# Pinned tiled runs in a chunked recurrence, and convolutions ahead of operand splits: one step of a hybrid decoder layer on one core

## The chip, the cores and the metric

The kernel runs on one core of one Trainium2 chip. The metric is the device time of one execution in microseconds, and the number that stands for a kernel is the median of its runs: 1178.71 us for the kernel before, from 3 runs between 1177.01 and 1179.49.

## The reference

One layer of a decoder is applied to a prompt of 512 tokens and to a sample group of 8 sequences with 8 tokens each, 576 tokens in all. Both groups use the same weights. Cut to its core:

```python
xn = rmsnorm(x, g_norm)
u, za, xb, zb, q, zc, gates = split_in(xn @ w_in)          # w_in: 1024 x 11392
oa, s_last, shift_last = rwkv7_branch(u, za, ...)          # 16 heads of 64
ob, h_last, conv_last = rglru_branch(xb, zb, ...)          # width 1024
oc = cross_attn(q, zc, mem_k, mem_v)                       # 4 heads, 256 memory tokens
g_a, g_b, g_c = split(sigmoid(gates), 3)
merged = g_a * (oa @ w_br_a) + g_b * (ob @ w_br_b) + g_c * (oc @ w_br_c)
y = x + merged @ w_out                                     # then a last rmsnorm
```

The RWKV-7 branch carries, for each head, a 64 x 64 state over the tokens:

```python
sa = einsum("bhvk,bhk->bhv", s, -kk_t)
s = s * w_t[:, :, None, :] + sa[..., None] * (kk_t * a_t)[:, :, None, :] + v_t[..., None] * k_t[:, :, None, :]
o_t = einsum("bhvk,bhk->bhv", s, r_t)
```

The RG-LRU branch is a convolution of width 4 over the tokens, two gates made by block-diagonal products of its result, and the scan h = a_t * h + b_t. The outputs are y for both groups, the last states, and the memory's keys and values.

## The kernel before

**Projections.** Every weight matrix is used in units of 128 columns (class Unit, L310). A unit's weights are loaded in one DMA of 512 KB (raw), rounded on ScalarE to a high part (whi, L293), and the rest is made on VectorE (wlo, L294). The activations xh and xl are split the same way, and a product is three matmuls: high by high, high by low, low by high. A unit is eight steps, one for each 128 rows of the contraction; a step for all tokens is six matmuls of 288 columns (L366 to L369). The class Stream (L318) holds the units in order. `st.go(n)` puts n steps into the program at that place, `st.until(label)` puts as many as are needed until that unit is through, and `st.add` puts units ahead of the others that wait. At the first step of a unit the next unit's weights are loaded. So the projections are the filler that is woven between everything else: u, k, r, v of the recurrence, its gate za, and a list of units whose results are put aside in DRAM (zb, g, xb, zc; L449).

**The order of the work.** The program is written in one order, and a scheduler then orders each engine's instructions from a model of their times: an instruction that is not ready in its model lets later ones go ahead. On TensorE, `K.mm` and `K.transpose` (L63, L69) can pin an instruction: while `K.pin` is set, each is held behind the instruction that was traced just before it on that engine. Before the change `K.pin` is set in `lru_phase` alone (L571 to L611), and the stream's steps, which use `K.mm` too, are pinned there with the rest. In the recurrence nothing is pinned, and most of its matmuls call `nc.tensor.matmul` directly.

**The recurrence** (`rwkv_phase`, L861) goes over four groups of two pairs of heads (G = 2, L863), and turns the token-by-token recurrence into nine chunks of 64 tokens, the ninth being the 64 sample tokens. Names, for one pair o:

- `prep_a` (L958) and `prep_b` (L985) make the decays and the scaled keys and reads, in tiles BK and ZR; `rs` (L991) is a row sum in column tiles.
- `prep_c` (L1022) scales BK to BKn by each chunk's decay, transposes v and BKn (`vt`, `bkt`, whole matmuls), and at its end makes the products M1 (`m`, L1049: tiles of 64 x 64 of the array, evacuated with a mask by VectorE at L1055).
- `invert` (L1059) sends the diagonal 32 x 32 blocks of M1 through DRAM (d1) to a layout in which VectorE inverts all of them at once by 30 substitution steps (L1072 to L1077), and sends the result back (d2, d3).
- `direct` (L1115) makes products that do not need the inverse (R, Zt); `bonus` (L1011) one more term.
- `invert2` (L1094) completes the inverse with tiles of 32 x 32 (`z`, `w`), `solved` (L1141) applies it (`U`, `W`, tiles of 64 x 64).
- `chain` (L1182) is one chunk: A, two whole matmuls from the state (L1187), VectorE's addition of A to UV (`plus_state`, L1177), dS (L1196) and the outputs (`outs`, L1167, which add to A), both in column tiles of 64, and VectorE's addition of dS to the state sbd (L1204). GpSimd scales the state for the next chunk meanwhile (L1189). Two steps of the stream are put after A and four after the outputs.
- `sample_a`, `sample_b`, `sample_c` (L1222 to L1272) treat the ninth chunk, with eight separate states: transposes of the loaded states (whole), A8 in column tiles of 32 (L1248) and dSs in column tiles of 64 (L1261), transposes and stores. They follow chunks 1 to 3 for the first pair and 4 to 6 for the second.

After chunk 7 come the za units, the group norm, `prep_a` of the next group, and the output of the branch.

**The LRU phase** (`lru_phase`, L482). Just before it, all eight tiles of the attention branch's output are loaded from DRAM (SyncE's queue) and split to high and low parts on ScalarE and VectorE (`load_split`, L474, called at L1512). Then, pinned: a convolution (`conv`, L502; its input xe comes by a DMA on ScalarE's queue, then one ScalarE and four VectorE passes), 8 steps, the next convolution, 6 steps, the first `gates` (`pg`, L531), and so on, until the last g unit is through; then the branch products (`br`) begin, first with the attention branch's split output.

The instructions of a float32 matmul are two in the profile, so the eight dS of a chunk are four matmuls.

Of the kernel before, what the change touches and what calls it, by code (L numbers as in the profile page):

```python
# [9 lines left out]
F32 = mybir.dt.float32  # L10
# [8 lines left out]
P = 128  # L19
D = 1024  # L20
KC = 8
# [296 lines left out]
class Stream:  # L318


    def __init__(self, K):
        self.K = K
        self.first, self.fill = [], []
        self.cur = self.nxt = None
        self.k = 0
        self.done = set()

# [15 lines left out]
    def step(self):  # L343
# [138 lines left out]
def lru_phase(K, o2, merge, operand):  # L482
# [6 lines left out]
    with tc.tile_pool(name="lruc", bufs=1, reuse_waits="tile") as lc, tc.tile_pool(name="lru", bufs=2, reuse_waits="tile") as lp:  # L489
# [121 lines left out]
        K.pin = False  # L611
# [249 lines left out]
def rwkv_phase(K):  # L861
# [5 lines left out]
    with ExitStack() as es:  # L867
# [90 lines left out]
        def prep_a(o):  # L958
# [5 lines left out]
            for s in range(2):  # L964
                cs = slice(HN * s, HN * s + HN)
                for n, (dst, bias) in enumerate(((tw, K.w0h), (ta, K.a0h))):
                    pl = K.psb("lora")[:, 0:HN]
                    nc.tensor.matmul(pl, wlh[:, n, :], xw2[n][:, cs], start=True, stop=False)
                    nc.tensor.matmul(pl, wll[:, n, :], xw2[n][:, cs], start=False, stop=True)
# [15 lines left out]
        def prep_b(o):  # L985
# [4 lines left out]
            for c in range(NCH):  # L990
                nc.tensor.matmul(pr_[br:br + 64, 2 * c:2 * c + 2], o.sq[:, C * c:C * c + C], K.bones2, start=True, stop=True,  # L991
                                 tile_position=(0, br))
# [18 lines left out]
        def bonus(o):  # L1011
# [3 lines left out]
            for s in range(2):  # L1015
                cs = slice(HN * s, HN * s + HN)
                pb = K.psb("bon")[:, 0:HN]
                nc.tensor.matmul(pb, K.bones, hi[:, cs], start=True, stop=False)
                nc.tensor.matmul(pb, K.bones, lo[:, cs], start=False, stop=True)
                nc.vector.tensor_mul(o.bon[:, cs], pb, o.v[:, cs])  # L1020

        def prep_c(o):  # L1022
            q, BK, ZR = o.q, o.BK, o.ZR
            rv = rsv[q]
            UV = o.UV = UV2[0][:, q]
            BKn = o.BKn = rg.tile([P, NCH, P], F32, tag="BKn", name="BKn")
            for c in range(8):
# [3 lines left out]
                                 o.Ps[:, :, NS:NS + 1].unsqueeze(1).to_broadcast([P, 2, NB, NS]))  # L1031
            for c0, n in ((0, 4), (4, 4), (8, 1)):
# [10 lines left out]
            M1 = o.M1 = rg.tile([P, H2, P], F32, tag="M1", name="M1")  # L1043
            for c0, n in ((0, 4), (4, 4), (8, 1)):
                pms = [K.psb("m1") for h in range(2)]
                for c in range(c0, c0 + n):
                    for w in range(2):
                        for h in range(2):
                            nc.tensor.matmul(pms[h][64 * w:64 * w + 64, P * (c - c0):P * (c - c0) + P],  # L1049
                                             BK[64 * h:64 * h + 64, c, w, :],  # L1050
                                             ZR[64 * h:64 * h + 64, c].rearrange("p a b -> p (a b)"), start=True, stop=True,
                                             tile_position=(64 * h, 64 * w))
                for h in range(2):
                    for c in range(c0, c0 + n):
                        nc.vector.scalar_tensor_tensor(M1[:, 2 * c + h, :], pms[h][:, P * (c - c0):P * (c - c0) + P],  # L1055
                                                       rv[:, c, h:h + 1], maskq[q][c == 8],
                                                       op0=ALU.mult, op1=ALU.mult)

        def invert(prs):  # L1059

            d1 = dr.tile([NQ, 32, 32], F32, tag="d1", name="d1")
            for blk in range(2):
                for o in prs:
                    q0 = (blk * G + o.q) * H2
                    nc.sync.dma_start(d1[q0:q0 + H2].rearrange("q s t -> s q t"),
                          o.M1[o.br + 32 * blk:o.br + 32 * blk + 32, :, o.br + 32 * blk:o.br + 32 * blk + 32])
# [3 lines left out]
            nc.sync.dma_start(X, d1)  # L1070
# [23 lines left out]
        def invert2(prs):  # L1094
            for g0 in (0, 9):
                pzs = [K.psb("z1") for o in prs]
                for g in range(g0, g0 + 9):
                    for o, pz in zip(prs, pzs):
                        a, b = o.br, o.br + 32
                        nc.tensor.matmul(pz[b:b + 32, 32 * (g - g0):32 * (g - g0) + 32], o.M1[a:a + 32, g, b:b + 32],  # L1100
                                         o.xz[a:a + 32, g, :], start=True, stop=True, tile_position=(a, b))
                for o, pz in zip(prs, pzs):
                    b = o.br + 32
                    nc.scalar.copy(o.xz[b:b + 32, g0:g0 + 9, :].rearrange("p a b -> p (a b)"), pz[b:b + 32, 0:288])
                pws = [K.psb("w12") for o in prs]
                for g in range(g0, g0 + 9):
                    for o, pw in zip(prs, pws):
                        a, b = o.br, o.br + 32
                        nc.tensor.matmul(pw[a:a + 32, 32 * (g - g0):32 * (g - g0) + 32], o.xz[b:b + 32, g, :],
                                         o.M1[b:b + 32, g, b:b + 32], start=True, stop=True, tile_position=(b, a))  # L1110
                for o, pw in zip(prs, pws):
                    a, b = o.br, o.br + 32
                    nc.scalar.copy(o.M1[a:a + 32, g0:g0 + 9, b:b + 32], pw[a:a + 32, 0:288].rearrange("p (a b) -> p a b", b=32))

        def direct(prs):  # L1115

            r0 = prs[0].r0 = [rt.tile([P, N], F32, tag="k", name="r0") for _ in range(2)]
            for c0, n in ((0, 4), (4, 4), (8, 1)):
                pR = K.psb("R")
                for c in range(c0, c0 + n):  # L1120
                    for h in range(2):
                        for o in prs:
                            a, b, m = o.kr, o.br, P * (c - c0) + C * h
                            nc.tensor.matmul(pR[b:b + 64, m:m + C], o.M1[a:a + 64, 2 * c + h, b:b + 64],
# [448 lines left out]
```

## Time and profile before

| What | Value |
|---|---|
| median of 3 runs | 1178.71 us |
| the profiled execution's own time | 1175.92 us |
| its span, first to last instruction | 1174.2 us |
| mean granted TensorE clock | 0.992 |
| TensorE matmul busy | 1135.5 us |
| VectorE busy | 709.0 us |
| ScalarE busy | 521.2 us |
| HBM read, written | 120.82 MB, 29.01 MB |

Engines are called PE (TensorE's matmuls), PEld (its weight loads), DVE (VectorE), ACT (ScalarE), POOL (GpSimd) and SP (SyncE); a q behind a name is the engine's sequencer, which issues DMAs. Rows of the timeline give the start in us from the span's start, the length in us, the engine, the line of the kernel, the operation, what it writes and reads, the rows and columns of the array that a matmul uses (128*128 is the whole array), its shape, and how many instructions of the kind follow one another. In square brackets stands the engine's idle time before, and what ended it. Matmuls overlap in TensorE's pipeline, so the pace is read from one start to the next, not from the lengths.

### The profile page before, as it was taken

The page shows a single profiled execution, that of the slowest core. Times are in us where ns is not written, and L with a number is a line of the kernel's source. Part 1 is how long each engine was busy: PE and PEld are TensorE (multiplying, and loading weights), DVE is VectorE, ACT ScalarE, POOL GpSimd, SP SyncE. Part 2 cuts the span into 40 slices and gives each one's busy share as a digit, 9 for nine tenths or more (in the row PEclk, how much of TensorE's full clock was granted, in tenths as well). Part 3 has the DMA queues.
Part 4 walks back from the last instruction along what each step waited for, and adds up shares of the span by engine and source line. Part 5 has one row for each costly group of instructions (what it writes and reads, how often), then busy time and mean ns, then how long its engine had stood idle before and what let it go on. Part 6 is the DMA issues. An engine that isn't in the chain of part 4 may idle for free.

```text
span 1174.2 us, 25723 instructions
## 1 busy us (share of the span) xinstructions
PE 1135.5 (97%) x10567; PEld 1064.0 (91%) x10567; DVE 709.0 (60%) x1454; ACT 521.2 (44%) x1004; POOL 148.0 (13%) x287
## 2 busy tenths in 40 slices
PE   6999999999999999999999999999999799999997
PEld 4998988899899899998899988989989799999997
DVE  5345655245883478745686745879445669684633
ACT  5454444245523365324472244642323677622333
POOL 3010000011002210003210022100121012020032
PEclk9999999999999999999999999999999899999999
DMA  5456757632334223352223423234544846566412
GB/s 141 130 198 198 223 181 233 199 101 64 95 116 113 73 66 91 109 152 55 65 86 101 132 76 76 76 97 127 139 114 136 261 134 206 151 218 179 126 37 81
DMA packets 220622, 151.49 MB, mean 129 GB/s; under 512 B 52640, under 2 KB 196106, under 8 KB 220506
## 3 DMA queue, kind: packets, MB, share of 16 engines
q1 hardware_dynamic: 217242, 146.87, 42.7%
q10 hardware_dynamic: 3264, 2.99, 0.9%
q8 instruction: 83, 1.36, 0.5%
q14 instruction: 33, 0.27, 0.1%
HBM read 120.82 MB, written 29.01 MB: 128 GB/s over the span
## 4 chain that ended last, share of the span: by engine, by line
PE 79%; DVE 6%; DMA 5%; ACT 5%; issue 4%; SPq 0%; POOL 0%; DVEq 0%; ACTq 0%; POOLq 0%
PE u L71 13%; PE g L71 12%; PE br L71 11%; PE xb L71 4%; PE za L71 4%; PE fo L71 4%; PE q L71 4%; PE zc L71 3%; PE zb L71 3%; PE kv L71 2%; PE pg L71 1%; PE m L1049 1%; DVE wlo L294 1%; PE dS L1196 1%; PE skt L65 1%
## 5 line engine op out<-in xcount | busy, mean ns | idle before, releaser
L293 ACT CAST whi<-wraw 128x1024 fp32r<-128x1024 f32 x129 | 135.2, 1048 | 313.8 <-PE g L71 91.1
L294 DVE TENSOR_TENSOR wlo<-wraw,whi 128x1024 fp32r<-128x1024 f32 x128 | 158.1, 1235 | 117.1 <-ACT whi L293 108.1
L71 PE MATMUL u<-xh,whi 128*128 128x288 f32 x400 | 92.5, 306 | 0.0
L71 PE MATMUL u<-xh,wlo 128*128 128x288 f32 x400 | 89.9, 301 | 0.0
L71 PE MATMUL u<-xl,whi 128*128 128x288 f32 x400 | 88.2, 300 | 0.0
L71 PE MATMUL g<-xh,whi 128*128 128x288 f32 x384 | 85.7, 304 | 0.0
L71 PE MATMUL g<-xl,whi 128*128 128x288 f32 x384 | 84.4, 300 | 0.0
L71 PE MATMUL g<-xh,wlo 128*128 128x288 f32 x384 | 84.1, 299 | 0.0
L71 PE MATMUL br<-oh,wlo 128*128 128x288 f32 x384 | 82.7, 297 | 1.4 <-DVE wlo L294 1.4
L71 PE MATMUL br<-oh,whi 128*128 128x288 f32 x384 | 83.6, 299 | 0.0
L71 PE MATMUL br<-ol,whi 128*128 128x288 f32 x384 | 82.3, 296 | 0.0
L71 PEld LDWEIGHTS u<-xh,whi 128*128 128x128 f32 x400 | 65.0, 188 | 6.2 <-issue 4.7
L71 PEld LDWEIGHTS u<-xh,wlo 128*128 128x128 f32 x400 | 65.1, 188 | 1.8 <-issue 0.8
L71 PEld LDWEIGHTS u<-xl,whi 128*128 128x128 f32 x400 | 64.6, 189 | 0.6 <-issue 0.2
L71 PEld LDWEIGHTS g<-xh,whi 128*128 128x128 f32 x384 | 62.4, 190 | 1.5 <-issue 1.0
L71 PEld LDWEIGHTS br<-oh,wlo 128*128 128x128 f32 x384 | 61.8, 189 | 1.9 <-DVE wlo L294 1.8
L71 PEld LDWEIGHTS g<-xh,wlo 128*128 128x128 f32 x384 | 62.4, 189 | 1.2 <-issue 1.2
L71 PEld LDWEIGHTS g<-xl,whi 128*128 128x128 f32 x384 | 62.4, 189 | 1.1 <-issue 1.0
L71 PEld LDWEIGHTS br<-oh,whi 128*128 128x128 f32 x384 | 62.2, 189 | 0.6
L71 PEld LDWEIGHTS br<-ol,whi 128*128 128x128 f32 x384 | 61.9, 189 | 0.0
L1075 DVE TENSOR_TENSOR Xt<-X 72x30 f32<-72x30 f32 (+14 forms) x120 | 39.3, 327 | 12.9 <-DMA X<-d 9.2
L71 PE MATMUL fo<-woh,oh 128*128 128x256 f32 (+1 forms) x160 | 44.9, 280 | 0.0
(392 smaller groups left out, 2856.4 us busy)
## 6 DMA issues: line engine op xcount, KB each, us to landing
wraw<-in_w_in SPq DMA_DIRECT2D x89, 512.0 KB
wraw<-in_w_mem_kv SPq DMA_DIRECT2D x16, 512.0 KB
kn<-in_cache_mem_k SPq DMA_DIRECT2D x16, 512.0 KB
kn<-in_cache_mem_v SPq DMA_DIRECT2D x16, 512.0 KB
gd<-flt SPq DMA_DIRECT2D x24, 288.0 KB
gtt<-gd SPq DMA_DIRECT2D x24, 288.0 KB
wraw<-in_w_br_c SPq DMA_DIRECT2D x8, 512.0 KB
wraw<-in_w_br_a SPq DMA_DIRECT2D x8, 512.0 KB
```

The lines of the kernel that those rows point to most:

```text
L65: ins = self.nc.tensor.transpose(out, in_, self.ident[:rows, :rows])
L71: ins = self.nc.tensor.matmul(*a, **kw)
L293: nc.scalar.copy(hi, raw)
L294: eng.tensor_sub(lo, raw, hi.bitcast(F32))
L1049: nc.tensor.matmul(pms[h][64 * w:64 * w + 64, P * (c - c0):P * (c - c0) + P], BK[64 * h:64 * h + 64, c, w, :], ZR[64 * h:64 * h + 64, c].r ...
L1075: nc.vector.tensor_mul(tv, X[:, 0:s, s:s + 1].to_broadcast([NQ, s, m]), X[:, s:s + 1, s + 1:].to_broadcast([NQ, s, m]))
L1196: nc.tensor.matmul(pS[hs, C * o.q:C * o.q + C], o.BKn[:, c, hs], o.UV[:, c, hs], start=True, stop=True, tile_position=(0, 64 * h))
```

## The change

In the recurrence:

- From `bonus` to the end of chunk 7, `K.pin` is set, and the recurrence's matmuls go through `K.mm`, so each is held behind what was traced just before it. The stream's steps have a pin of their own, `st.pin`, which is set only in the LRU phase.
- `chain` takes two functions. `full()` is traced behind A: the sample's transposes. `tiled()` is traced behind the outputs: A8, the sample's outputs and dSs. The sample's parts move by that: its outputs and dSs stand a chunk behind A8, its states are loaded ahead of chunk 0 and behind chunk 3, and `sample_c` of the second pair comes after chunk 7.
- The steps in a chunk are 2 and 4 as before, but 1 and 3 in the last group.
- `prep_c` is cut in three. `scaled` (BKn) and `products` (M1, and the DMA of its blocks to d1, per pair) come right behind `prep_b`; the transposes come behind the load of the blocks, and then the substitution, `direct`, 26 steps, the next group's units, 10 steps and `bonus`. Before it was 37 steps behind `bonus`, and the next group's units came behind `solved`.
- In `invert2` both halves of z come first, one step, both halves of w, three steps.

In the LRU phase, the load and split of the attention branch's output are cut in four pieces of two tiles, behind the first three convolutions and the second gates.

```diff
@@ class Stream @@
+        self.pin = False
...
-                K.mm(self.ps[:, o:o + m], a[:, k, :], b[:, k, t0:t0 + m],
-                                 start=(k == 0 and q == 0), stop=(k == KC - 1 and q == 2))
+                ins = nc.tensor.matmul(self.ps[:, o:o + m], a[:, k, :], b[:, k, t0:t0 + m],
+                                       start=(k == 0 and q == 0), stop=(k == KC - 1 and q == 2))
+                if self.pin:
+                    K.tc.keep_in_program_order(ins)
@@ lru_phase @@
-        K.pin = True
+        K.pin = st.pin = True
         conv(0)
+        load_c(range(0, 2))
         st.go(8)
         conv(1)
+        load_c(range(2, 4))
         st.go(6)
         gates(0)
         conv(2)
+        load_c(range(4, 6))
         st.go(5)
         gates(1)
+        load_c(range(6, 8))
         st.until("g17")
@@ rwkv_phase: products @@
+            for blk in range(2):
+                q0 = (blk * G + q) * H2
+                a = o.br + 32 * blk
+                nc.sync.dma_start(d1[0][q0:q0 + H2].rearrange("q s t -> s q t"), o.M1[a:a + 32, :, a:a + 32])
@@ invert2 @@
+            half(0)
+            half(9)
+            st.go(1)
+            above(0)
+            above(9)
+            st.go(3)
@@ chain @@
-        def chain(os, c):
+        def chain(os, c, steps, full, tiled):
...
                 plus_state(os, c, pA)
-                st.go(2)
+            full()
+            if c > 0:
+                st.go(steps[0])
...
             outs(os, c, pA, c == 0)
             for o in os:
                 o.cur = nxt[:, o.q, :]
-            st.go(4)
+            tiled()
+            st.go(steps[1])
@@ the loop over groups @@
             for o in prs:
                 prep_b(o)
                 st.go(3)
-            UV2[0] = rg.tile([P, G, NCH, P], F32, tag="UV", name="UV", bufs=1)
+                scaled(o)
+                products(o)
+                st.go(3)
+            X = invert()
             for o in prs:
                 prep_c(o)
-                st.go(6)
-            invert(prs)
+                st.go(3)
+            substitute(prs, X)
             direct(prs)
+            st.go(26)
+            if g + 1 < NG:
+                st.add(*group_units(g + 1))
+            st.go(10)
+            K.pin = True
             for o in prs:
                 bonus(o)
-            st.go(37)
             invert2(prs)
             solved(prs)
             if g + 1 < NG:
                 lora_w(g + 1)
-                st.add(*group_units(g + 1))
+            o0, o1 = prs
+            none = lambda: None
+            fulls = {1: lambda: sample_a(o0), 4: lambda: sample_c(o0), 5: lambda: sample_a(o1)}
+            tileds = {2: lambda: sample_b(o0), 3: lambda: [sample_o(o0), sample_in(o1)],
+                      6: lambda: sample_b(o1), 7: lambda: sample_o(o1)}
+            sample_in(o0)
             for c in range(8):
-                chain(prs, c)
-                if c in (1, 4):
-                    sample_a(prs[c // 4])
-                if c in (2, 5):
-                    sample_b(prs[c // 4])
-                if c in (3, 6):
-                    sample_c(prs[c // 4])
+                chain(prs, c, (2, 4) if g + 1 < NG else (1, 3), fulls.get(c, none), tileds.get(c, none))
+            K.pin = False
+            sample_c(o1)
@@ hybrid_step @@
-    load_split(K, o2, K.ocz, *oc)
...
-    ob, lru_rows = lru_phase(K, o2, merge, operand)
+    ob, lru_rows = lru_phase(K, o2, lambda ks: load_split(K, o2, K.ocz, *oc, ks), merge, operand)
```

`sample_o` is the sample's outputs and dSs with VectorE's addition, taken out of `sample_b` and `sample_c`; `sample_in` is the load of the states, taken out of `sample_a`.

More of the change, by code (lines that the diff above doesn't have):

```diff
@@ L1031, in prep_c, with products @@
                                  o.Ps[:, :, NS:NS + 1].unsqueeze(1).to_broadcast([P, 2, NB, NS]))
+        def products(o):
+            q, BK, ZR = o.q, o.BK, o.ZR
+            rv = rsv[q]
+            M1 = o.M1 = rg.tile([P, H2, P], F32, tag="M1", name="M1")
+            for c0, n in ((0, 4), (4, 4), (8, 1)):
+                pms = [K.psb("m1") for h in range(2)]
+                for c in range(c0, c0 + n):
+                    for w in range(2):
+                        for h in range(2):
+                            K.mm(pms[h][64 * w:64 * w + 64, P * (c - c0):P * (c - c0) + P],
+                                             BK[64 * h:64 * h + 64, c, w, :],
+                                             ZR[64 * h:64 * h + 64, c].rearrange("p a b -> p (a b)"), start=True, stop=True,
+                                             tile_position=(64 * h, 64 * w))
+                for h in range(2):
+                    for c in range(c0, c0 + n):
+                        nc.vector.scalar_tensor_tensor(M1[:, 2 * c + h, :], pms[h][:, P * (c - c0):P * (c - c0) + P],
+                                                       rv[:, c, h:h + 1], maskq[q][c == 8],
+                                                       op0=ALU.mult, op1=ALU.mult)
+            for blk in range(2):
+                q0 = (blk * G + q) * H2
+                a = o.br + 32 * blk
+                nc.sync.dma_start(d1[0][q0:q0 + H2].rearrange("q s t -> s q t"), o.M1[a:a + 32, :, a:a + 32])
+        def prep_c(o):
+            rv = rsv[o.q]
+            UV = o.UV = UV2[0][:, o.q]
+            BKn = o.BKn
             for c0, n in ((0, 4), (4, 4), (8, 1)):
@@ L1042, in prep_c, with invert @@
                                      rv[:, c0:c0 + n, :].rearrange("p c h -> p (c h)").unsqueeze(2).to_broadcast([P, 2 * n, C]))
[L1043 to L1066, printed above, removed]
+        def invert():
             X = rg.tile([P, NCH, 2, C], F32, tag="BK", name="X").rearrange("p a b c -> p (a b c)")
@@ L1094, in invert2, with half @@
         def invert2(prs):
-            for g0 in (0, 9):
+            def half(g0):
                 pzs = [K.psb("z1") for o in prs]
@@ L1195, in chain @@
                     hs = slice(C * h, C * h + C)
-                    nc.tensor.matmul(pS[hs, C * o.q:C * o.q + C], o.BKn[:, c, hs], o.UV[:, c, hs], start=True, stop=True,
-                                     tile_position=(0, 64 * h))
+                    K.mm(pS[hs, C * o.q:C * o.q + C], o.BKn[:, c, hs], o.UV[:, c, hs], start=True, stop=True,
+                         tile_position=(0, 64 * h))
             pS3 = pS[:, 0:G * C].rearrange("p (q v) -> p q v", v=C)
@@ L1260, in sample_c @@
                 hs = slice(C * h, C * h + C)
-                nc.tensor.matmul(pS[hs].rearrange("p (b v) -> p b v", v=C), o.BKn[:, 8, hs], o.uvx[:, :, hs],
-                                 start=True, stop=True, tile_position=(0, 64 * h))
+                K.mm(pS[hs].rearrange("p (b v) -> p b v", v=C), o.BKn[:, 8, hs], o.uvx[:, :, hs],
+                     start=True, stop=True, tile_position=(0, 64 * h))
             nc.vector.tensor_add(s1, s1, pS.rearrange("p (b v) -> p b v", v=C))
+        def sample_c(o):
+            s1 = o.s1
             so = big("so")[:, 0:4, :]
@@ L1338, in rwkv_phase @@
         for g in range(NG):
+            UV2[0] = rg.tile([P, G, NCH, P], F32, tag="UV", name="UV", bufs=1)
+            d1[0] = dr.tile([NQ, 32, 32], F32, tag="d1", name="d1")
             for o in prs:
```

67 lines of the change are left out of this document (36 added, 31 removed).

## The prediction

> **What bounds the kernel now.** I read the page first, then the stretches of the four recurrence groups, then TensorE's own order of time inside one group, then the stretch where the LRU branch starts.
>
> ```profile
> span 1174.2 us, 25723 instructions
> ...
> PE 1135.5 (97%) x10567; PEld 1064.0 (91%) x10567; DVE 709.0 (60%) x1454; ACT 521.2 (44%) x1004; POOL 148.0 (13%) x287
> ...
> PE 79%; DVE 6%; DMA 5%; ACT 5%; issue 4%; SPq 0%; POOL 0%; DVEq 0%; ACTq 0%; POOLq 0%
> ```
>
> TensorE is the bound: busy 97% of the span, and 79% of the chain that ended last. A change can gain by taking away TensorE's idle time, or time in which it counts as busy but does not move at its pace. The change removes no matmul, so the second kind has to be looked for in the recurrence.
>
> ```profile
> 446.00:600.30 154.30, 152.91 (x1645) 142.29 (x1643) 101.58 (x234) 68.31 (x143) 23.22 (x37) 1.00 0.34 93
> 600.30:755.80 155.50, 153.69 (x1656) 143.06 (x1656) 103.02 (x234) 69.36 (x150) 22.80 (x47) 1.00 0.34 93
> 755.80:910.40 154.60, 152.21 (x1643) 141.36 (x1642) 100.56 (x224) 56.05 (x112) 16.67 (x21) 1.00 0.44 124
> ```
>
> The columns are the stretch, its length, then busy time of PE, PEld, DVE, ACT, POOL, the clock, and DMA. These are the last three groups of two head pairs. TensorE idles 154.30 - 152.91 = 1.39, 1.81 and 2.39 us in them, 5.6 us together. Waiting is not what the recurrence loses by.
>
> **What a change of tile shape costs.** TensorE in order of time, inside the third group:
>
> ```profile
> 702.64 0.45 PE L1196 MATMUL dS<-UV,BKn 128*64 128x64 f32 x8
> 702.92 0.40 PE L1172 MATMUL A<-UV,M 128*64 128x64 f32 x8
> 703.26 0.53 PE L71 MATMUL u<-xh,whi 128*128 128x288 f32 x2
> ...
> 710.46 0.61 PE L1187 MATMUL A<-sbd,ZR 128*128 128x128 f32 x4
> 710.82 0.51 PE L71 MATMUL u<-xl,whi 128*128 128x288 f32 x2
> ...
> 711.53 0.34 PE L1196 MATMUL dS<-UV,BKn 128*64 128x64 f32 x4
> 711.79 0.40 PE L71 MATMUL u<-xh,whi 128*128 128x288 f32 x1
> 712.12 0.34 PE L1196 MATMUL dS<-UV,BKn 128*64 128x64 f32 x4
> 712.29 0.40 PE L1172 MATMUL A<-UV,M 128*64 128x64 f32 x8
> 712.62 0.40 PE L71 MATMUL u<-xh,whi 128*128 128x288 f32 x1
> ...
> 713.49 1.08 PE L1248 MATMUL A<-sbs,zx 128*32 128x128 f32 x32
> 714.50 0.38 PE L1187 MATMUL A<-sbd,ZR 128*128 128x128 f32 x1
> ```
>
> ```profile
> 634.85 36.79 PE xb L71 x276
> ```
>
> Undisturbed, projection matmuls go at 36.79 / 276 = 0.133 us each (the second row, from the chain that ended last). In one chunk the eight dS and the eight output instructions stand together: from 702.64 to the next projection at 703.26, 0.62 us. In the next chunk one projection matmul lies between the two pairs' dS: 711.53 to 712.62, 1.09 us, of which 0.133 is that matmul. One split therefore costs 1.09 - 0.133 - 0.62 = 0.34 us, all of it counted as busy. How often does it happen?
>
> ```profile
> 600.31 1.21 PE L991 MATMUL rs<-bones,sq 128*64 128x2 f32 x18
> ```
>
> ```profile
> 671.97 0.75 PE L1100 MATMUL z<-xz,M 32*32 32x32 f32 x18
> ...
> 726.93 0.34 PE L1196 MATMUL dS<-UV,BKn 128*64 128x64 f32 x4
> ```
>
> From 600.31 to 726.93 I counted 31 runs of tiled matmuls with whole ones between: 9 until the triangular inverse's second half starts at 671.97, 5 from there through U, W and chunk 0, and 17 for chunks 1 to 7.
>
> **The change part by part.**
>
> Runs kept together. As written, chunks 1 to 7 need one tiled run each (7 for 17), and the inverse needs z, w, and U to chunk 0 (3 for 5); the 9 before are as they were. That is 12 fewer of 31 in each of four groups: 48 x 0.34 = 16.3 us at most. I don't take all of it, because the projection steps stay free: only the recurrence's own matmuls are pinned behind what was traced before them. The row of 276 matmuls is 46 steps of six, where the code writes 37 between the products and z. So the scheduler, finding z not ready, pulls later steps forward, and it can still do so. Products first starts the DVE substitution some 4 us (5 steps) sooner by the DVE work that it passes, so about 46 - 36 - 5 = 5 steps of later slots still go early; filling the inverse's latencies takes some 3 more than are written there. With 8 steps used up, a chunk runs at its latency and has a step fall between its two dS, as at 711.79, until the six steps a chunk have caught up, some three chunks. So 9 of 12 go: 36 x 0.34 = 12.2 us. The low end is 4 a group, 16 x 0.34 = 5.4 us; the high end 16.3.
>
> Of these runs some hold two shapes, since the sample's A8 (32 columns) is put next to outputs of 64 columns.
>
> ```profile
> 872.10 1.08 PE L1248 MATMUL A<-sbs,zx 128*32 128x128 f32 x32
> 873.11 0.53 PE L71 MATMUL zc<-xl,whi 128*128 128x288 f32 x2
> ```
>
> A8 takes 1.01 us here, where outputs of 64 columns stand just ahead of it, and 1.01 us at 713.49, where whole matmuls do. [...]
>
> New waits on TensorE. A pinned matmul whose operand is late holds the pinned ones behind it. In a chunk, A must be read and added by DVE before dS:
>
> ```profile
> 711.11 0.61 DVE L1180 TENSOR_TENSOR UV<-A,UV 64x128 f32<-64x128 f32 x2 [3.56 <-PE A L1187]
> ```
>
> ```profile
> PE dS L1196 <- DVE UV L1180: 1.9, 7, 0.5
> ```
>
> From the start of A at 710.46 to the end of both adds at 711.72 is 1.26 us. Two written steps (12 x 0.133 = 1.6 us) cover it; in the last group one step (0.8 us) and A's own run just about do. dS to the state's add is as long, against four or three steps. Queued behind a waiting dS are the outputs, the sample's products and the next chunk's A; ACT's copies of the outputs and GpSimd's scaling of the state wait with them. Today dS waits 1.9 us in seven cases, 0.27 each, over all groups. Bounds for the 28 chunks: none and 28 x 0.27 = 7.6 us, or a gain of 2 if waits like today's go. I take +2, near today's row.
>
> Products first, the block's DMA issued per pair, the next group's u units added 10 steps before the inverse, the sample's state load ahead of chunk 0: no work is added. They move DMAs on SP's queue past the weight loads; TensorE has 54 written steps (43 us) between preparation and z as cover, as before. I cost them at nothing; without that cover z would be late by the 4 us that products first gains. The eleven steps less in the last group's chain (four more in its inverse) go to the LRU's start: moved, not removed.
>
> The LRU's start. Now eight loads and splits of the attention branch stand ahead of the first convolution, and TensorE reaches the gate products (pg) before their input:
>
> ```profile
> 921.80:928.20 6.40, 0.04 (x1) 0.00 (x0) 5.17 (x8) 3.77 (x5) 0.35 (x2) 0.66 1.03 356
> 928.20:931.85 3.65, 3.57 (x9) 2.60 (x9) 2.92 (x5) 1.05 (x3) 0.02 (x1) 0.50 0.78 247
> 931.85:937.10 5.25, 5.25 (x33) 5.11 (x32) 3.76 (x6) 4.70 (x8) 0.33 (x2) 0.79 0.43 104
> ```
>
> TensorE does nothing for 6.36 us, and then works at a clock of 0.50 for 3.65 us and 0.79 for 5.25 us: 3.65 x 0.50 + 5.25 x 0.21 = 2.9 us more. Together 9.3 us.
>
> ```profile
> 918.73 0.32 POOL L506 COPY conv_st<-xe 128x3 f32<-128x3 f32 x1 [13.70 <-DMA xe<-xbd]
> ```
>
> ```profile
> 925.25 0.76 DVE L628 TENSOR_TENSOR ol<-oxl,oh 128x576 fp32r<-128x576 f32 x1 [1.20 <-ACT oh L627]
> 925.93 1.59 DVE L513 SCALAR_TENSOR_TENSOR cva<-xe,par,cva 128x600 f32<-128x600 f32 x2
> 927.44 0.75 DVE L515 SCALAR_TENSOR_TENSOR xc<-xe,par,cva 128x512 f32<-128x512 f32 x1
> 928.10 0.28 DVE L517 SCALAR_TENSOR_TENSOR xc<-xe,par,cva 128x64 f32<-128x64 f32 x1
> ```
>
> The input xe is there at 918.73; the convolution's end on DVE is 928.38, since its passes stand in DVE's queue behind splits (ol), one of which waited 1.20 us for its own operand. Without them the convolution takes one ACT and two DVE passes (0.80 each, by the 1.59 for two) and 0.75 + 0.28: 3.4 us, so 922.1 even if xe comes no sooner, against 921.8. What is left is 0.3 to nothing, so 9 of 9.3 us go. The other bound: the scheduler still lets some splits pass ahead, and half stays: 4.6. [...]
>
> The splits, now in four pieces of two tiles, come as late as behind the second gates; their ACT and DVE passes are hidden by the g steps still to run before the first branch product, more of them than before by the eleven moved here (66 x 0.133 = 8.8 us). Nothing taken; up to 3 us if they are late.
>
> The sum: -12.2 + 2 - 9 = -19.2 us. The profiled execution took 1175.92 us, 1.7 over its span of 1174.2, so it would take 1156.7. The median of the runs is 1178.71, 2.8 above the profiled one; the change is the same amount on that, 1159.5 us.
>
> **The rivals.**
>
> Only the LRU gains. The steps are free, so whole matmuls keep falling between tiled ones, and the edit doesn't do what its words say. For it: 46 steps ran where 37 were written. Against: dS, outputs and A8 are now each chained to the one before, and nothing is pulled between two that are both ready. Time: 1178.7 - 9 = 1169.7, 1171 with some of the new waits.
>
> The wait moves to the branch products. The splits come behind gates, and the first branch product waits in the LRU's place. For it: ACT and DVE are in use there (4.70 and 3.76 of 5.25 us). Against: the 8.8 us of moved steps. Time: 1178.7 - 12.2 + 2 = 1168.5.
>
> Slower. Free steps run ahead everywhere, so that none is left between a pinned A and its dS, and TensorE waits out DVE's latency in every chunk: 1.26 us less A's own 0.36 (710.46 to 710.82), 0.9 us. At 28 chunks this is 25 us, against 21 gained: +4, 1182.7. It decides from 21.2 / 28 = 0.76 us a chunk. Against it: the scheduler, where it sees such a wait, has always found a later step to put there; idle time of 5.6 us in three groups shows that its picture of DVE holds on the chip.
>
> **How the numbers follow.** Forecast 0.62, only LRU 0.20, moved wait 0.09, slower 0.09. A measurement of this kernel can tell 0.2%, 2.4 us. The first three cases are faster by more, save for 0.04 of them where the low ends meet; of the slower case 0.01 ends within 0.2%. So faster 0.87, same 0.05, slower 0.08. Bounds: all high ends give -16.3 - 2 - 9.3 = -27.6, 1151; all low ends -5.4 + 7.6 - 4.6 + 3 = +0.6, 1179. The range goes from 1151 to 1173: it takes in the forecast but for its worst corner, the second and third case, and leaves out the slower one.
>
> **What would show it.** Right: no idle time before pg and a clock of 1.00 through that stretch; 20 to 24 tiled runs a group; groups of 151 to 152 us for the same matmuls; each dS of the later chunks in one run of eight with its outputs. Wrong: 28 or more runs a group; waits of PE dS or PE A of over 7 us in all; a new wait of PE br on a split; a group longer than 154 us.

## The result, and the profile after

| | time, median of its runs | against the kernel before |
|---|---|---|
| before | 1179.10 us (6 runs) | |
| after | 1171.01 us (1163.77 to 1174.65, 6 runs) | ratio 0.9931, 95% interval 0.991 to 0.9952 |

The change gains 8 us of the 19.2 forecast. The profiled execution of after took 1170.21 us with a span of 1168.5, against 1175.92 and 1174.2 before. A row of the page after, and the same stretches as before (length, busy PE, PEld, DVE, ACT, POOL, clock, DMA share, GB/s); the first three rows are the last three groups, the others the LRU's start:

```profile
PE 1126.0 (96%) x10567; PEld 1059.1 (91%) x10567; DVE 707.3 (61%) x1454; ACT 522.6 (45%) x1004; POOL 159.3 (14%) x287
```

```profile
436.30:590.50 154.20, 150.28 (x1656) 140.41 (x1655) 102.54 (x234) 69.16 (x143) 25.23 (x36) 1.00 0.34 94
590.50:747.70 157.20, 153.49 (x1657) 143.39 (x1656) 101.93 (x234) 69.79 (x150) 27.84 (x50) 0.98 0.34 92
747.70:900.70 153.00, 150.37 (x1636) 140.74 (x1636) 102.40 (x226) 55.42 (x112) 21.77 (x22) 0.98 0.45 125
...
912.20:916.16 3.96, 0.10 (x1) 0.03 (x1) 2.32 (x4) 2.53 (x4) 0.35 (x2) 0.87 1.08 366
916.16:919.73 3.57, 3.57 (x9) 2.57 (x9) 3.51 (x6) 2.33 (x5) 0.43 (x2) 0.50 0.50 161
919.73:924.95 5.22, 5.22 (x33) 5.08 (x32) 3.56 (x6) 4.76 (x9) 0.16 (x1) 0.79 0.75 223
```

The second group before, cut in the same way, from its first matmul to the next group's:

```profile
445.20:600.30 155.10, 153.71 (x1656) 143.09 (x1655) 102.38 (x234) 69.11 (x143) 23.22 (x37) 1.00 0.34 93
```

Three things are to be seen. In the second group TensorE is busy for 150.28 us where it was 153.71 for as many instructions, so the matmuls do go faster; but it idles 154.20 - 150.28 = 3.92 us where it idled 1.39. The third and fourth group have a clock of 0.98, where all four had 1.00 in the profiled execution before. And the LRU's start still has its wait, though a shorter one: 3.86 us idle, then 3.57 us at a clock of 0.50.

TensorE in order of time, in one of the later chunks of the third group:

```profile
703.48 0.43 PE L369 MATMUL u<-xh,wlo 128*128 128x288 f32 x2
703.83 0.45 PE L71 MATMUL dS<-UV,BKn 128*64 128x64 f32 x8
704.11 0.40 PE L71 MATMUL A<-UV,M 128*64 128x64 f32 x8
704.45 0.53 PE L369 MATMUL u<-xh,whi 128*128 128x288 f32 x2
```

Both pairs' dS and outputs stand in one run of 704.45 - 703.83 = 0.62 us, as forecast. Counted in one way for both kernels, the groups had 32, 31, 31 and 30 tiled runs and have 23, 23, 24 and 24: 30 fewer. What TensorE waits for inside the four groups, after (in us, times, longest):

```profile
PE m L71 <- DVE M L1054: 5.7, 7, 1.2
PE ot L65 <- ACT flt L419: 2.3, 2, 1.2
PE ot L65 <- DVE onat L1325: 1.6, 2, 1.1
```

The waits of dS for UV, 1.9 us before, are gone from the list. The products m wait 5.7 us for DVE's M (L1054, which moves them out of PSUM), where they waited 2.5.

Such a wait stands in this place, in the preparation of the third group. The stretches are cut where the record of the granted clock changes, and one step of 3.41 us ahead of it:

```profile
605.95 0.44 PE L71 MATMUL m<-ZR,BK 64*64 64x128 f32 x4 [1.16 <-DVE M L1054]
```

```profile
604.50:607.90 3.40, 2.24 (x28) 1.53 (x20) 3.40 (x15) 1.41 (x4) 0.00 (x0) 1.00 0.58 158
607.90:614.70 6.80, 6.80 (x39) 6.51 (x38) 4.90 (x13) 2.45 (x3) 0.00 (x0) 0.50 0.18 52
```

TensorE waits 1.16 us for M in the first stretch, in which it is busy 2.24 of 3.40 us. In the 6.80 us behind it the clock is 0.50 (a half-clock stretch, as it is called below), though TensorE is busy throughout: up to 6.80 x 0.50 = 3.4 us are lost to the clock behind a wait of 1.16. The fourth group has the same:

```profile
761.50:764.90 3.40, 2.24 (x34) 1.52 (x23) 3.40 (x14) 1.57 (x5) 0.00 (x0) 1.00 0.46 133
764.90:771.70 6.80, 6.80 (x39) 6.51 (x38) 4.77 (x13) 2.51 (x4) 1.31 (x1) 0.50 0.17 58
```

From one half-clock stretch to the next it is 764.9 - 607.9 = 157.0 = 46 x 3.413 us, and from there to the one at the LRU's start 915.1 - 764.9 = 150.2 = 44 x 3.413. From 607.92 on the record of the clock has stretches of 6.83, 150.19, 6.83, 143.36, 6.83 and 242.35 us, which are 2, 44, 2, 42, 2 and 71 times 3.413: its changes lie on a grid of 3.413 us, and so do those of before, with stretches of 3.41, 897.71, 10.24 and 235.52 us (1, 263, 3 and 69). The six runs of after have mean clocks of 0.985 to 0.996, and their times go with them: 1163.77 us at 0.996, 1174.65 at 0.985.

At the LRU's start, DVE after (GpSimd's copy of the first input, which shows that it has landed, runs at 907.11):

```profile
909.85 0.76 DVE L635 TENSOR_TENSOR ol<-oxl,oh 128x576 fp32r<-128x576 f32 x1 [4.04 <-ACT oh L634]
910.65 0.84 DVE L516 SCALAR_TENSOR_TENSOR cva<-xe,par,cva 128x600 f32<-128x600 f32 x1
911.41 0.75 DVE L635 TENSOR_TENSOR ol<-oxl,oh 128x576 fp32r<-128x576 f32 x1
912.08 0.84 DVE L516 SCALAR_TENSOR_TENSOR cva<-xe,par,cva 128x600 f32<-128x600 f32 x1
914.55 0.84 DVE L516 SCALAR_TENSOR_TENSOR cva<-xe,par,cva 128x600 f32<-128x600 f32 x1 [1.64 <-ACT cva L514]
915.32 0.75 DVE L518 SCALAR_TENSOR_TENSOR xc<-xe,par,cva 128x512 f32<-128x512 f32 x1
915.98 0.28 DVE L520 SCALAR_TENSOR_TENSOR xc<-xe,par,cva 128x64 f32<-128x64 f32 x1
```

The last cva (914.55) belongs to the second convolution: it waits for that one's input, and the first convolution's last passes (xc) stand behind it. Two splits (ol) still stand ahead of and between the first one's passes. The code puts the convolution first; the queues, ordered by the scheduler, don't. From the landing at 907.11 to the convolution's end at 915.98 + 0.28 = 916.26 it is 9.15 us, 3.4 by the forecast.

The theory that was tested: the recurrence's gain is real, but products first adds waits that cost their own length and, by the grid, the clock behind them; and the LRU's gain was not taken, because DVE's order holds the first convolution. Its rivals: a split is cheap, so there was little to gain; the chaining itself brings the waits; the convolution waits for its transfer.

### The profile page after: what moved, and what is told of

Same layout as the page of the kernel before. It is cut to its first block, busy times and chain, and to the rows that moved or that the text cites. A ratio compares the mean times of both kernels' runs of the same rounds, so it can differ in the third digit from the quotient of the medians.

```text
span 1168.5 us, 25699 instructions
## 1 busy us (share of the span) xinstructions
PE 1126.0 (96%) x10567; PEld 1059.1 (91%) x10567; DVE 707.3 (61%) x1454; ACT 522.6 (45%) x1004; POOL 159.3 (14%) x287
## 3 DMA queue, kind: packets, MB, share of 16 engines
q8 instruction: 83, 1.36, 0.5%
## 4 chain that ended last, share of the span: by engine, by line
PE 80%; DVE 7%; DMA 5%; ACT 4%; issue 3%; SPq 0%; POOL 0%; ACTq 0%; DVEq 0%; POOLq 0%
PE u L369 13%; PE g L369 12%; PE br L369 12%; PE za L369 4%; PE zc L369 4%; PE fo L71 4%; PE xb L369 4%; PE q L369 4%; PE kv L369 3%; PE zb L369 2%; PE A L71 2%; PE pg L71 1%; PE skt L65 1%; PE m L71 1%; PE dS L71 1%
## 5 line engine op out<-in xcount | busy, mean ns | idle before, releaser
L1272 POOL TENSOR_TENSOR zx<-ZR,bm 128x256 f32<-128x256 f32 x16 | 20.4, 1283 | 220.5 <-DVE X L1094 138.4
```

The lines of the kernel that those rows point to most:

```text
L1272: nc.gpsimd.tensor_mul(zx[:, w], o.ZR[:, 8, w, :].rearrange("p (g t) -> p g t", g=2).unsqueeze(2).to_broadcast([P, 2, 4, 32]), K.bm4.unsqu ...
```

## The experiments

Each kernel was timed beside the kernel before; its ratio to that (95% interval) is what is compared.

**The LRU's part alone.** The kernel before, with

```
         conv(0)
+        load_c(range(0, 2))
         st.go(8)
         conv(1)
+        load_c(range(2, 4))
```

and so on, and without the eight splits ahead.

> The kernel before with the LRU's part alone: eight splits in pieces of two behind the convolutions and gates, the recurrence untouched. As predicted, 9 of the 9.3 us at the LRU's start go: about 1170. The theory formed from the profile after: DVE takes conv 1's first pass ahead of conv 0's last ones and waits there for conv 1's input, so 3 to 4 us of idle time and most of the slow clock stay: 2 to 4 us less than the kernel before, about 1176. A rival, that the splits were never what held the convolution, expects no difference.

1176.95 us, ratio 0.9989 (0.9972 to 1.0006). TensorE idles 3.5 us before pg, as the theory said, but of its 2 to 4 us no difference can be told: 1.3 us by the ratio, 3.3 at the interval's end. The 9 us of the prediction are excluded. The recurrence is untouched here, and yet its profile has a half-clock stretch in the third group, behind a step in which TensorE did not wait at all:

```profile
679.60:683.00 3.40, 3.40 (x95) 3.01 (x95) 0.00 (x0) 1.56 (x4) 0.00 (x0) 1.00 1.04 288
683.00:686.40 3.40, 3.40 (x68) 3.36 (x66) 0.68 (x1) 0.97 (x2) 0.00 (x0) 0.51 0.00 0
```

The 95 matmuls are nearly all 32x32 (z and w). So the recurrence as it was could meet one too, and not only behind a wait.

**The recurrence's part alone.** After, with `load_split(K, o2, K.ocz, *oc)` ahead of the LRU as before.

> The changed kernel with all eight splits ahead of the convolutions, as before: the recurrence's part alone. As predicted, -12.2 + 2 us: about 1169. The theory from the profile after: 30 fewer tiled runs at 0.34 us (-10.2) are paid back by 6 us of new waits in the preparation and by half-clock stretches of up to 3.4 us each: 2 to 6 us less than the kernel before, 1173 to 1177, with a granted clock under 0.99. A rival, that a split costs 0.1 us and not 0.34, expects the same time but no half-clock stretch inside the groups.

1174.98 us, ratio 0.9962 (0.9937 to 0.9986), 4.5 us by the ratio, as the theory expected. Its twelve runs lie in two bunches: three at 1166.2 to 1167.2 with a clock of 0.995, nine at 1173.4 to 1180.0 with 0.982 to 0.988. Its profiled execution was one of the first bunch, without a half-clock stretch in a group, and shows what the change gives where none comes. Its third and fourth group:

```profile
590.60:744.80 154.20, 150.28 (x1656) 140.49 (x1655) 101.89 (x234) 69.81 (x150) 26.88 (x50) 1.00 0.34 94
744.80:895.40 150.60, 147.58 (x1636) 137.96 (x1636) 102.53 (x226) 55.50 (x112) 21.86 (x22) 1.00 0.46 127
```

With the same matmuls and waits, these two are 154.20 and 150.60 us where after has 157.20 and 153.00: 5.4 us, the two half-clock stretches. The time beyond 0.1333 us a projection matmul, all four groups together, was 202.6 us before and is 194.2 here: -8.4, of which idle time is +7.6 (7.9 to 15.5 us) and busy time -16.0.

**The old order of the preparation.** After, with

```
             for o in prs:
                 prep_b(o)
                 st.go(3)
+            for o in prs:
                 scaled(o)
+                prep_c(o)
                 products(o)
-                st.go(3)
+                st.go(6)
             X = invert()
```

> The changed kernel with the preparation in the old order (both pairs' first part, then scaling, transposes and products), the pinned recurrence and the LRU kept. Theory: the long waits of m for DVE's M and the half-clock stretches inside the groups go, 30 fewer tiled runs stay: 4 to 8 us less than the changed kernel, 1163 to 1167, clock 0.99 or more, and the groups' non-step time at about 204 us in place of 209.6. Rival (the pinned order itself brings the waits, or a split is cheap): within 2 us of the changed kernel.

1164.59 us, ratio 0.989 (0.9867 to 0.9913): 1.1% less than before where after has 0.7%. Its waits in the groups, and its second and third group:

```profile
PE m L71 <- DVE M L1054: 2.5, 4, 0.6
```

```profile
436.90:590.20 153.30, 150.65 (x1656) 140.96 (x1655) 101.82 (x234) 68.90 (x143) 22.15 (x36) 1.00 0.34 94
590.20:743.50 153.30, 150.42 (x1657) 141.02 (x1656) 101.51 (x234) 69.27 (x150) 24.95 (x50) 1.00 0.35 94
```

The long waits of m are gone, the clock is 1.00 in both groups (the first group has one half-clock stretch, shown further down) and its six runs have 0.990 to 0.995. The groups' time beyond the projection is 193.5 us, 198.9 in after: 5.4 us, 5.6 expected (there from another count of projection matmuls). The two intervals just touch, so the runs alone hardly tell the two kernels apart; the waits and the stretches do. So it is products first that cost, and not the chaining.

**The convolution's instructions kept in order, first try.** After, with ACT's and DVE's instructions of the first three convolutions and of the splits each queued behind the one traced just before on its engine.

> The changed kernel with ACT's and DVE's instructions of the first three convolutions and of the splits kept in their written order, so that conv 0's last passes no longer stand behind conv 1's first. Theory: no idle time before pg and a clock of 1.00 there, 3.9 + 2.9 = 6.8 us less than the changed kernel, about 1164. Rival (the first convolution is late because its input's DMA is slow beside the others): less than 1.5 us.

1168.47 us, ratio 0.9913 (0.9878 to 0.9947). The profile shows 4.5 us idle before pg, and the same order of DVE. The edit did not do what its heading says: each instruction is tied to its neighbour alone, and conv 1's first pass was tied to a weight split, which floats itself. So it tells nothing of the theory.

**No chaining.** After, without `K.pin = True` around the recurrence.

> The changed kernel without the chaining of the recurrence's matmuls: the new order is written as it is, but each matmul may float as before. If the chaining is what keeps the runs together (as predicted): about 31 tiled runs a group again, 30 more in all at 0.34 us, 1.5 to 2.5 us a group more than the changed kernel at an equal clock, 1176 to 1181. If the written order alone does it: 22 to 25 runs a group as in the changed kernel and the same time within 2 us.

1169.04 us, ratio 0.9926 (0.9911 to 0.9941), with 21, 22, 21 and 24 tiled runs. The forecast's mechanism falls: the written order alone gives the fewer runs. But at a clock of 1.00 its second and third group take 155.1 and 155.0 us, and with the chaining 154.2. Where the difference lies is seen in groups of instructions (busy us, mean ns of one) of before, of this kernel and of after, between 287 and 911 us:

```profile
L1109 PE MATMUL w<-M,xz 32*32 32x32 f32 x288 | 12.0, 192 | 0.0
L1248 PE MATMUL A<-sbs,zx 128*32 128x128 f32 x256 | 10.2, 277 | 0.0
L1100 PE MATMUL z<-xz,M 32*32 32x32 f32 x288 | 9.0, 192 | 0.0
```

```profile
L71 PE MATMUL A<-sbs,zx 128*32 128x128 f32 x256 | 10.2, 276 | 0.0
L71 PE MATMUL w<-M,xz 32*32 32x32 f32 x288 | 8.3, 192 | 0.0
L71 PE MATMUL z<-xz,M 32*32 32x32 f32 x288 | 8.3, 192 | 0.0
```

```profile
L71 PE MATMUL A<-sbs,zx 128*32 128x128 f32 x256 | 8.6, 276 | 0.0
L71 PE MATMUL z<-xz,M 32*32 32x32 f32 x288 | 6.3, 192 | 0.0
L71 PE MATMUL w<-M,xz 32*32 32x32 f32 x288 | 6.3, 192 | 0.0
```

One matmul takes as long in all three, 192 ns in z and w and 276 or 277 in A; only how they overlap differs. Unchained, the scheduler issues nine z of one pair (18 instructions, 32 ns from one start to the next) and then nine of the other, and by the code all nine lie on one tile of the array; chained, the pairs alternate, as written, between two tiles, with starts 7 and 25 ns apart in turn. That is 8.3 us against 6.3 for the same 288 instructions.

**Only the order inside the runs.** The kernel without chaining, with `K.pin` set around the matmuls of z, of w and of the sample's A.

> The kernel without the chaining, but with the 32x32 products of the inverse (z, w) and the sample's A of 32 columns chained again, so that the two pairs alternate inside a run. Theory: this order inside the runs is what the chaining is worth: z 7.2 to 5.7 us, w 7.4 to 6.2 us, the sample's A 9.4 to 8.1 us, so about 4 us less than the kernel without chaining at an equal clock, 1164 to 1166 if no half-clock stretch comes in. Rival (the chaining works through the chunks' dS and outputs): these three as short, but under 1 us less in all.

1170.06 us, ratio 0.9931 (0.9912 to 0.995): not 1164 to 1166. Its z, w and A are as short as chained, but its profile has one half-clock stretch in the second group. At full clock its four groups have 194.7 us beyond the projection (3.4 of one stretch taken off), against 198.4 without chaining and 194.2 chained: the 3.7 us are there, and its runs (0.989 to 0.994, against 0.991 to 0.996) give about as much back.

**A projection step inside the products.** After, with one of the three steps behind each pair's products moved ahead of their third part, and chained there (the pin is taken off again behind the products):

```
+                if c0 == 8:
+                    K.pin = st.pin = True
+                    st.go(1)
```

> The changed kernel with one projection step (six matmuls, 0.8 us) put inside each pair's products, ahead of the third part, in place of one of the three behind it: the place where TensorE waited 1.16 us for DVE's M. No work added. Theory: that wait goes, no clock of one half inside groups 2 to 4, and the runs of this kernel lie closer together: 1164 to 1167 with a clock of 0.990 or more. Rival (the waits only move to the next reader of a PSUM bank, or the half-clock stretches have another cause): within 2 us of the changed kernel, clock 0.985 to 0.99 in most runs.

1176.44 us, ratio 0.9988 (0.9976 to 1.0): slower than after, and neither expectation. The waits of m for M fall to 2.4 us, but

```profile
PE g L369 <- DVE flt L427: 5.5, 2, 2.9
PE m L71 <- DVE BK L1014: 4.2, 4, 1.2
```

The step is now chained between products, so it, and all that is queued behind it, wait for the unit before it to be moved out of PSUM, and the products for their own operands. What is shown is only that a chained step costs more here than the wait that it fills.

**The first convolution ahead.** After, with everything else that is traced for ACT and DVE up to the first gates queued behind its last instruction on each:

```
-        conv(0)
         load_c(range(0, 2))
-        st.go(8)
-        conv(1)
+        st.go(1)
+        c0, c1 = conv(0)
+        with tc.issue_after(c0), tc.issue_after(c1):
+            st.go(7)
+            conv(1)
```

> The changed kernel with ACT's and DVE's later work at the LRU's start queued behind all of the first convolution (one step, with its weight load, is taken ahead of it; the first two splits are ahead too). Theory: the convolution ends at about 3.4 us after its input lands, ahead of TensorE; no idle time before pg, a clock of 1.00 there, 6 to 7 us less than the changed kernel at equal stretches elsewhere: 1163 to 1166. Rival (what is queued behind it then holds TensorE as long, at the next g unit or at the second gates): less than 2 us.

1164.28 us, ratio 0.9884 (0.9857 to 0.991), in spite of a clock of 0.986 in its profiled run, with a half-clock stretch in each of the four groups. The LRU's start:

```profile
913.32 1.72 DVE L516 SCALAR_TENSOR_TENSOR cva<-xe,par,cva 128x600 f32<-128x600 f32 x2 [2.02 <-ACT cva L514]
915.07 0.75 DVE L518 SCALAR_TENSOR_TENSOR xc<-xe,par,cva 128x512 f32<-128x512 f32 x1
915.74 0.28 DVE L520 SCALAR_TENSOR_TENSOR xc<-xe,par,cva 128x64 f32<-128x64 f32 x1
```

```profile
912.40:916.00 3.60, 3.60 (x29) 3.60 (x28) 2.61 (x5) 2.10 (x3) 0.35 (x2) 1.00 0.91 275
916.00:922.00 6.00, 6.00 (x41) 5.58 (x40) 3.65 (x6) 3.53 (x6) 0.36 (x2) 1.00 1.01 347
```

The input lands at 912.4, and the convolution ends at 916.02: 3.6 us, 3.4 by the forecast. No idle time in these two stretches, and a clock of 1.00. From ro (a small transpose that stands just ahead of the LRU in every version) to the first branch product it is 30.4 us, against 36.6 after: 6.2 us. The transfer, the rival, was not what held it.

**The same without the recurrence's part.** The LRU's part alone, with the first convolution ahead.

> The kernel before with the LRU's part alone, and the first convolution ahead of ACT's and DVE's later work; the recurrence untouched. If the 9 us of the prediction are there but were only not taken, 6.5 to 9 us less than the kernel before: 1168.5 to 1171.5, no idle time over 1 us and a clock of 1.00 ahead of pg. Rival (only with the moved projection steps is there cover for the convolution): 3 to 5 us of idle time stay, 1173 to 1176.

1176.78 us, ratio 0.9987 (0.9973 to 1.0001). The convolution is in time, but

```profile
PE br L71 <- ACT whi L293: 4.1, 1, 4.1
PE pg L71 <- DVE xc L515: 0.5, 1, 0.5
```

Now the first branch product waits 4.1 us for the split of its weights, so the time that was won is lost again. Here are 160 matmuls of 288 columns between ro and br, and 208 in after: the 8 steps that the change leaves over from the last group (48 x 0.133 = 6.4 us) are the cover. My rival of the wait that moves to the branch products is what happens without them.

**Useless work in the place of the wait.** After, with two matmuls per pair that nothing reads, into banks that the real products overwrite:

```
                 pms = [K.psb("m1") for h in range(2)]
+                if c0 == 4:
+                    fl = ZR[:, 0:4].rearrange("p c a b -> p (c a b)")
+                    K.mm(pms[0], BK[:, 0]..., fl, start=True, stop=True)
+                    K.mm(pms[1][:, 0:P], BK[:, 0]..., fl[:, 0:P], start=True, stop=True)
```

> The changed kernel with useless work added: two matmuls per pair (128 rows, 512 and 128 columns, about 1.05 us) into the PSUM banks of the products' second part, overwritten by the real ones, so that TensorE is busy where it waited for DVE's M. Theory: the wait of 1.16 us was paid anyway, so the work costs little (under 0.5 us a pair), but no half-clock stretch follows: in spite of 8.5 us more work no slower than the changed kernel, 1166 to 1171, clock 0.990 or more in nearly all runs. Rival (the half-clock stretches have nothing to do with the wait): clock 0.985 to 0.99 as before and 2 to 8 us more time.

1168.9 us over five executions, ratio 0.9923 (0.9897 to 0.9949); one more, of 6074 us, is a disturbance and left out. Its groups of m:

```profile
L71 PE MATMUL m<-ZR,BK 64*64 64x128 f32 x576 | 23.8, 277 | 2.8 <-DVE M L1058 2.0 <-DVE BK L1014 0.6
L71 PE MATMUL m<-ZR,BK 128*128 128x512 f32 x16 | 9.0, 645 | 0.0
L71 PE MATMUL m<-ZR,BK 128*128 128x128 f32 x16 | 3.1, 274 | 0.0
```

The useless matmuls take 10.2 us of TensorE from start to start, the waits of m for M fall from 5.7 to 2.0 us, and the kernel is no slower. All five executions have a clock of 0.994 to 0.998; after, with the waits, reaches 0.994 in one of six, and the recurrence alone in three of twelve. The profile has no half-clock stretch in a group. So the stretches of 6.8 us come from the wait. Not all of the higher clock does: in this profile 3.38 us of idle time ahead of pg brought no half-clock stretch either, where 3.86 us in after brought one of 6.8 us. They lie across two steps of the grid, busy for 1.60 and 1.82 of 3.40 us.

**Both steps together.** The step inside the products, with the first convolution ahead.

> Both edits together, the step inside the products and the first convolution ahead. If both theories hold, the gains add: 4 to 7 and 6 to 7 us less than the changed kernel, 1156 to 1161, clock 0.993 or more.

1170.03 us, ratio 0.9931 (0.9913 to 0.995), not 1156 to 1161. The convolution's gain is there once more (6.4 us less than with the step alone), the step's loss as well.

**Both mended.** The old order of the preparation, with the first convolution ahead.

> The changed kernel with both places mended: the preparation in its old order, and the first convolution ahead of ACT's and DVE's later work. The two gains measured apart, 6.4 us and 6.7 us, lie in different stretches and should add: 1157 to 1160, faster than both kernels. If the half-clock stretches only move on (to z and w, which now stand together in the first group), 1160 to 1164.

1160.75 us, ratio 0.9864 (0.9842 to 0.9886), clocks of 0.992 to 0.996: the fastest version here, with its whole interval below after's. It is 0.8 us over its first expectation and in the second's range; its profile has one half-clock stretch in the groups, of 3.4 us, at z and w in the first group, where the second named it. Of the two gains over after, 0.41 and 0.47%, 0.67 are there together.

## Why the prediction was wrong

Profiled execution against profiled execution the miss is 19.2 - 5.7 = 13.5 us. Of the signs that were named, the 20 to 24 runs a group came, and so did the later dS in one run; the idle time before pg, and groups of more than 154 us, spoke against it. Point by point:

**Runs kept together, -12.2.** The number held (30 fewer, 36 forecast; chunks 3 to 7 clean, the first ones split, as argued), and the gain was larger: TensorE's busy time in the groups fell by 16.0 us where the clock held. Some 6.8 us of it (start to start: z 7.55 to 5.69, w 9.84 to 6.24, the sample's A 9.40 to 8.09 us) are z, w and A overlapping better, which I had not seen; the other 9.2 us would be 0.31 us for each of 30 runs, near my 0.34, if all the rest is put down to them; the same working gives 8.9 us for 36 runs, 0.25 us each, in the kernel without chaining. The reason was wrong: the chaining does not make the runs, the written order does; the chaining makes the order inside them.

**New waits, +2.** The waits that I looked at, dS for UV, went away. Idle time grew all the same, by 6.3 us in after's groups (7.9 to 14.2): about 3.8 in m, in the preparation, where I had not looked, and 2.3 in ot, the transposes of a group's outputs (1.6 before, 3.9 after), which was not followed up.

**Products first, costed at nothing: the step that failed.** I named 54 written steps as cover for the inverse, and did not ask what the products themselves wait for. DVE has a weight split and a product (wlo, 1.22 us, and BKn, 0.28 us) ahead of M; the products of the first eight chunks, two tiles for each four of them, fill the four PSUM buffers, and the ninth chunk's products wait for the first to come free. Before, other matmuls stood there. This is +3.2 us in m's waits for M, and by the clock about 6 us more in the profiled execution (busy time fell 10.0 us in after, 16.0 in the profile without such stretches).

The length of the gap alone does not tell what it costs: a gap of 1.16 us was enough, with TensorE busy for 2.24 of 3.40 us, and one of 3.38 us, across two steps, brought nothing in the kernel with the useless work.

**The LRU's start, -9.** It gave 2.6. The step that failed is "9 of 9.3 us go": I took the splits for what held the convolution, while any later work that the scheduler thinks ready can, such as conv 1's first pass. My lower bound, 4.6, held half for certain and was not low enough. With the queues in order it gives 2.6 + 6.2 = 8.8 us, but only with the 8 moved steps (11 forecast) as cover, which I had called worth nothing to the sum.

**The splits late, 0 to +3.** Nothing: from the first branch product to the end it is 231.2 us in both.

Together, in the profiles: groups -16.0 + 6.0 + 6.3 = -3.7, the LRU -2.6, the start of the kernel +0.5: -5.8 of the -5.7 measured. With both failed steps mended the kernel is at -1.36%, or -16 us, which the forecast's terms nearly give.

Why does the wait cost the clock at one time and not at another? The kernels that keep it (after, the recurrence alone, the first try at the convolution, no chaining, the order inside the runs, the first convolution ahead) have together 18 waits of 1.16 us in groups two to four of their profiles. A half-clock stretch of 6.8 us follows eight of them, those that begin 0.06 to 0.56 us into a step of the grid; none follows the other ten, which begin 0.70 to 3.35 us into one (the steps are counted from the changes of the clock in the same profile). So in these eighteen the place on the grid decides. The kernel without chaining met no stretch in its profile, and its three waits begin 0.70, 1.21 and 2.64 us into a step. A group with such a stretch is 157.2 us long, 46.06 steps of the grid, so the next group's wait falls on nearly the same place: 0.22, 0.39 and 0.56 us in the kernel with the first convolution ahead. Without one it is 154.2 us, 45.2 steps: 2.15, 2.73 and 3.35 us in the recurrence alone.

What stays open is what else must come together for a half-clock stretch. The same share of busy time was passed over in the kernel without chaining:

```profile
451.40:454.80 3.40, 2.25 (x56) 1.77 (x44) 3.40 (x11) 2.34 (x7) 0.00 (x0) 1.00 0.27 84
454.80:461.60 6.80, 6.80 (x64) 6.21 (x64) 6.30 (x16) 2.45 (x3) 1.58 (x1) 1.00 0.41 111
```

There 56 matmuls fell into the stretch of the grid, where the ones before half-clock stretches held 28 and 34. But the number does not decide either:

```profile
366.20:369.60 3.40, 3.15 (x140) 2.64 (x140) 0.00 (x0) 2.72 (x8) 0.32 (x2) 1.00 0.42 101
369.60:373.00 3.40, 3.40 (x75) 3.34 (x70) 0.40 (x1) 2.09 (x5) 0.00 (x0) 0.51 0.98 270
```

In the first group of the kernel with the old preparation, 140 matmuls of mostly 32x32 were followed by 0.51. So neither busy time nor count decides alone, and no run here shows what does.

## What to carry to other kernels

Look at idle time by place, not as a sum: here eight waits of 1.16 us, on a TensorE that was busy for the other 2.24 of a step's 3.40 us, were followed by 6.8 us at a clock of 0.50, and all eight began in the first 0.56 us of a step of the clock's grid; ten that began later were not. So ask of a moved step not only who needs it, but what it now waits for itself and whether other matmuls stand in that gap. A line put first in the code is not first in an engine's queue: read the queue's order around it, and tie what must not pass. And where small matmuls can alternate between two tiles of the array, the order inside a run can be worth nearly as much as the number of runs (6.8 us here, and 9.2).

## What the runs showed of the hardware

In the profiles of before and after, the granted clock changes on a grid of 3.413 us. Half-clock stretches in the groups were 3.4 or 6.8 us long. In the six kernels that keep the wait, eight of 6.8 us followed a wait of 1.16 us that began 0.06 to 0.56 us into a step of the grid, with TensorE busy for 2.24 or 2.25 of 3.40 us in the five of them in after and in the first convolution ahead; ten such waits that began 0.70 us or more into one were followed by none. Two of 3.4 us (the old preparation, and the LRU's part alone) followed steps in which TensorE was busy for 3.15 and 3.40 of 3.40 us, when nearly all matmuls were 32x32 tiles. Executions of one kernel, the first try at the convolution, differ by up to 14.9 us (1161.64 to 1176.54), and their mean clock (0.996 and 0.985) goes with it. 288 instructions of 32x32 products take 8.3 us when nine products in a row use one tile, and 6.3 us when two tiles alternate, at 192 ns each in both.
